# Two-layer trunk on one core: which splits stand behind tile 3's rows, and when the adaLN sums are split and multiplied

## The chip, the cores and the metric

One Trainium2 chip, one core. The metric is the device time of one execution in microseconds; before the change it is 1136.38 us (median of 3 runs, 1134.65 to 1137.98).

## What is computed

512 tokens of width 1024 pass through two layers, each a token mixer and then a SwiGLU feed-forward block (FFN):

```python
for i in range(2):
    shift, scale, gate = split(silu(c) @ mix_ada_w[i] + mix_ada_b[i], 3)
    h = rms_norm(x, mix_pre_g[i]) * (1 + scale) + shift
    y = stick_breaking_mixer(h) if i == 0 else token_mixing_mixer(h)   # attention / gMLP
    x = x + gate * rms_norm(y, mix_post_g[i])
    shift, scale, gate = split(silu(c) @ ffn_ada_w[i] + ffn_ada_b[i], 3)
    h = rms_norm(x, ffn_pre_g[i]) * (1 + scale) + shift
    y = (silu(h @ w_gate[i]) * (h @ w_up[i])) @ w_down[i]              # 1024 -> 2816 -> 1024
    x = x + gate * rms_norm(y, ffn_post_g[i])
```

Attention is stage 0, the first FFN stage 1 (FFN0 below), the gMLP stage 2, the second FFN stage 3 (FFN1). `shift`, `scale` and `gate` of a stage (the adaLN sums) are called `B`, `A` and `G` in the kernel. They hang on `c` alone and can be made at any time before the stage that uses them.

## The kernel before

**Arithmetic.** Every product runs in a rounded fp32 format. Each operand is split into a high and a low part: ACT writes the high part (`wh`, `as`, `hTh`, `acch`, with a copy), DVE writes the low part (`wl`, `hTl`, `accl`, with a subtraction of the two). `mm3` issues three matmuls, high x high, high x low, low x high. All matmuls are on line 88, transposes on 96, DVE and ACT instructions on 64, loads on 105, so groups are told apart by the names of their tiles.

**Tiling.** Tokens go in four tiles of 128 (0 to 3). In FFN0 and FFN1 the gate and up products run first, one unit of 128 hidden columns after another (`unit`, line 1022, for the first three units; `seven`, line 1040, for the other 19, a block scheme with 7 products whose weights are 2x2 block sums made in `blocks`, line 164). Then comes the down product, `out_proj` (line 468): k runs over 22 chunks of 128 hidden columns. Steps k = 0 to 17 do all four tiles, each step 24 matmuls of 128x512; the last four chunks (the tail) are done tile by tile, so that each tile's boundary can begin.

**Boundary.** `boundary` (line 395) turns one tile of `y` into the next stage's input: square sums on ACT, `t = y*G` and `x = t*r + x` on DVE, the new x out to DRAM, a square sum of x on ACT (`junk`), `t = x*A`, `t = t*r + B` on DVE, then eight transposes on TensorE (`tp<-pack,t`) and the splits of the transposed tile (`hTh`, `hTl`). Beside tiles 2 and 3 the first three units of the next stage (`nxt`, of two token tiles) are issued, so that TensorE has products while the boundary runs; the third (`nxt[2]`) is written after tile 3's boundary.

**adaLN sums.** `Bg` (line 295) is a generator. For each part (`A1`, `B1`, `G2`, ...) it loads eight 512 KB chunks of the adaLN weights (`rawada`) through a pool of two buffers on the SP queue and adds each to an accumulator 128x1024 on DVE (`A<-rawada,sc,A` and so on). Then, part by part and half by half (128x512), the accumulator is split (`acch`, `accl`), multiplied with a matrix of ones on TensorE into a PSUM bank (`adaps`), and evacuated back into the accumulator, with a gain vector `g` for A and G. A load is issued on SP only after the DVE instruction that frees its buffer, so it holds up the loads queued behind it. In FFN0's down product `bg` does two additions a step and the whole second half (`bg.step(99)`) at k = 12, for `A1`, `B1`, `G2`. At that point tile 0's running sum is put away in `yp`, and tile 0's two PSUM banks are given to `adaps`: from k = 13 tile 0 begins again (`y_` names with a new number), to be added to `yp` later. `bg2` makes `A2` and `B2`: their sums begin at k = 13 and are finished in the gMLP.

**What sets the order.** Behind the attention stage the instructions of each engine are ordered by the tile framework's scheduler: roughly in the order in which the program writes them, moved up where buffers are free. Buffers of the pool `s4` (28 slots of 4 KB a partition: x, sums, activations, `act`, and the split activations `as` of the down product) are handed out in the order in which the program asks. The weights of the down product go through six pairs `wh`, `wl` (pools of 5 and 1) and two raw buffers; a pair is written for step k + 6 when the last matmul of step k has read it.

Names and lines that the change touches: `Written` (55), `blocks` (164), `Bg` (295 to 363), `boundary` (395), `sums`, `out_proj` (468), `Ffn.first` (1022), and the place where `bg2` and `f0.run` are called.

Of the kernel before, what the change touches and what calls it, by code (L numbers as in the profile page):

```python
# [11 lines left out]
ALU = mybir.AluOpType  # L12
# [13 lines left out]
def trunk(ctx: ExitStack, tc: tile.TileContext, A: dict, out: bass.AP):  # L26
# [16 lines left out]
    def nm(s):  # L43
        uid[0] += 1
        return f"{s}_{uid[0]}"
# [9 lines left out]
    class Written:  # L55

        def __init__(self, engine):
            self.engine, self.prev, self.chain = engine, None, False

        def __getattr__(self, name):  # L60
            f = getattr(self.engine, name)

            def call(*a, **k):
                b = f(*a, **k)  # L64
                if self.chain and self.prev is not None:
                    order(b, self.prev)
                self.prev = b
                return b

            return call  # L70
# [97 lines left out]
    def blocks(xr, yr):  # L168

        fp = fwork["pool"]  # L170
        x = wtile(KD, P)
        split(x[0][:], x[1][:], xr[:])
        b21 = [fp.tile([P, 4, P], F32R, tag=f"b21{i}", name=nm("b21")) for i in range(2)]
        split(b21[0][:], b21[1][:], yr[:, 0:4, :])
        f13 = fp.tile([P, KD, P], F32, tag="f13", name=nm("f13"))
        dve.tensor_tensor(
            f13[:].rearrange("p (a k) f -> p a (k f)", a=2),
            xr[:].rearrange("p (a k) f -> p a (k f)", a=2),
            yr[:, 4:8, :].rearrange("p (a k) f -> p a (k f)", a=1).to_broadcast([P, 2, 512]),
            ALU.add,  # L180
        )
        t13 = wtile(KD, P)
        split(t13[0][:], t13[1][:], f13[:])
        f24 = fp.tile([P, KD, P], F32, tag="f24", bufs=1, name=nm("f24"))
        dve.tensor_tensor(f24[:, 0:4, :], f13[:, 0:4, :], xr[:, 4:8, :], ALU.add)
        dve.tensor_tensor(f24[:, 4:8, :], f24[:, 0:4, :], yr[:, 0:4, :], ALU.add)
        t24 = wtile(KD, P)
        split(t24[0][:], t24[1][:], f24[:])

        def half(t, i):  # L190
            return lambda k: (t[0][:, 4 * i + k, :], t[1][:, 4 * i + k, :])

        return {
            "B11": half(x, 0), "B22": half(x, 1), "B21": half(b21, 0),
            "T1": half(t13, 0), "T3": half(t13, 1), "T2": half(t24, 0), "T4": half(t24, 1),
        }
# [92 lines left out]
            acc, w, sc[:, kk : kk + 1], acc, ALU.mult, ALU.add  # L289
        )  # L290

    ada = {}

    class Bg:

# [1 line left out]

        def __init__(self, *parts, slots=False, queue=nc.sync):  # L300
            self.slots = slots
# [17 lines left out]
        def run(self):  # L319
            for name, at, s, part in self.parts:  # L320
                acc = slot(F32, name, 1, D)[:, 0, :]
                ada[name, at] = acc
                nc.gpsimd.memset(acc, 0.0)
                load(acc[0:1, :], A["adab"][s, part], self.queue)
                for k in range(KD):
                    if self.slots:
                        raw = slot(F32, "rawada", 1, D)[:, 0, :]
                        load(raw, A["ada"][s, part, k])
                        yield
                    else:  # L330
                        self.ahead(1 + (k + 1 < KD or name != self.parts[-1][0]))
                        raw = self.raws.pop(0)
                    ada_stt(acc, raw, k)
                    if not self.slots:
                        yield
            for name, at, s, part in self.parts:
                acc = ada[name, at]
                if part:
                    row = A["pre_g"] if part == 1 else A["post_g"]
                    g = slot(F32, "g", 1, D)[:, 0, :]  # L340
                    load(g, row[s : s + 1, :].to_broadcast([P, D]))
                for b in range(2):
                    c = slice(b * 512, (b + 1) * 512)
                    h = adas.tile([P, 512], F32R, tag="acch", name=nm("acch"))
                    l = adas.tile([P, 512], F32R, tag="accl", name=nm("accl"))
                    split(h[:], l[:], acc[:, c])
                    yield
                    yield
                    ps = self.bank()
                    mm(ps[:], ones_r, h[:], True, False, last_tp[0])  # L350
                    mm(ps[:], ones_r, l[:], False, True)
                    if part == 0:
                        act.activation(acc[:, c], ps[:], AF.Copy)
                    elif part == 1:
                        dve.scalar_tensor_tensor(acc[:, c], ps[:], 1.0, g[:, c], ALU.add, ALU.mult)
                    else:
                        dve.tensor_tensor(acc[:, c], ps[:], g[:, c], ALU.mult)

        def step(self, n=1):

# [30 lines left out]
    def boundary(s, tt, y, xin, hT, S, tag):  # L391
# [21 lines left out]
        sd, r1 = rms(sx[:])  # L413
        dve.tensor_tensor(t[:], x[:], ada["A", s], ALU.mult)
        dve.reciprocal(r1[:], sd[:])
        dve.scalar_tensor_tensor(t[:], t[:], r1[:, 0:1], ada["B", s], ALU.mult, ALU.add)
        late = []
        for q in range(2):
            ps = bank("tp", tag)
            for k in range(4):  # L420
                kk = q * 4 + k
                transpose(ps[:, k * P : (k + 1) * P], t[:, kk * P : (kk + 1) * P])
            a = ps[:].rearrange("p (a b) -> p a b", a=4)
            if tt % 2 == 0:
# [8 lines left out]
            late.append(a)  # L433
        return lambda: sums(S, tt, late)

    def sums(S, tt, a):

# [19 lines left out]
        part("3", f[:, 0])  # L457

    xd = {}

    def x_load(tt):

# [5 lines left out]
    def out_proj(s, nk, get_act, wkey, J, bg, hT, nxt=(), pre=None, S=None, steps=0, bg2=None):  # L468
# [23 lines left out]
        if pre is not None:  # L492
            npre = len(pre["w"])
            for tt in pre["y"]:
                y[tt] = pre["y"][tt]
        for k in range(nk - J):
            a = get_act(k)
            w = pre["w"][k] if k < npre else wget(wkey(k))
            for tt in range(NT):
                if k >= npre or tt not in pre["y"]:  # L500
                    step(k, tt, a, w)
            bg.step(steps)
            if bg2 is not None and mid is not None and k >= mid:
                bg2.step(1)
            if k + 1 == mid:
                yp = slot(F32, "yp")
                for hf in range(2):
                    act.activation(yp[:, hf, :], y[last][hf][:], AF.Copy)
                bg.step(99)
        bg.step(99)  # L510
        tail = [
            (k, get_act(k), wget(wkey(k), J + 1 if k == nk - J else 0))
# [17 lines left out]
        for n, tt in enumerate((2, 3)):  # L530
            if nxt:
                evacs.append(nxt[n]())
            late.append(boundary(s, tt, y[tt], xin, hT, S, "p" if tt == 3 else "b"))
        if nxt:
            evacs.append(nxt[2]())
            with tc.issue_after(last_sqrt[0].ins):
                for f in evacs:
                    f()
        if hT is not None:
            for f in late:  # L540
                f()

    def sqrt_table():
        with tc.issue_after(last_act[0].ins):
# [445 lines left out]
    class Ffn:  # L990
# [29 lines left out]
            return evac  # L1020

        def first(self):
            return [lambda f=f: self.unit(f, 0, 256, 2) for f in range(NH)]

        def seven(self, f):

# [90 lines left out]
    def gmlp(bg, hT, nhT, nS, nxt):  # L1117
# [112 lines left out]
        0, KD, lambda k: (o8[k][:, 0, :], o8[k][:, 1, :]), lambda k: ("wo", k),  # L1230
        4, bg, hT1, f0.first(), early, S1,
    )
    bg2 = Bg("A2", "B2")
    f0.run(
        Bg("G1", slots=True), Bg("A1", "B1", "G2"), bg2, 2, hT2,
        [lambda a=a: u_first(hT2, range(a, min(a + 2, NU))) for a in range(0, NU, 2)],
    )
    gmlp(bg2, hT2, hT3, S3, f1.first())
# [86 lines left out]
```

## Time and profile before

| what | value |
|---|---|
| median of 3 runs | 1136.38 us (1134.65 to 1137.98) |
| the profiled execution, its own time | 1136.57 us |
| its span in the profile | 1134.7 us |
| PE busy | 98% of the span |
| DVE, ACT, POOL busy | 74%, 51%, 4% |
| mean granted TensorE clock | 0.999 |

The profile is of one execution. Times in it are microseconds from the span's start; the execution's own time is 1.9 us longer than the span. A row of the timeline gives start, length, engine, line, instruction and tiles, how many such followed each other, and in brackets the idle time of the engine before it with what ended it.

### The profile page before, as it was taken

What the parts mean: (1) busy time and instruction counts of PE and PEld (TensorE: products, weight loads), DVE (VectorE), ACT (ScalarE), POOL (GpSimd) and SP (SyncE); (2) the same over time, 40 slices, a digit from 0 to 9 for tenths busy, and PEclk for the clock granted to TensorE, in tenths of its full rate; (3) what the DMA queues carried; (4) which work ended last, traced back from release to release, by engine and by line L of the source; (5) the groups of instructions that cost most, each with busy time, mean ns of one, the idle gap of its engine ahead of it and who ended that gap; (6) DMA issues with size and microseconds to landing.
All of it is one profiled execution on the core that took longest, in us unless ns stands there. A gap on an engine that the chain in (4) does not pass through costs nothing.

```text
span 1134.7 us, 17753 instructions
## 1 busy us (share of the span) xinstructions
PE 1114.4 (98%) x7120; PEld 989.6 (87%) x7120; DVE 842.1 (74%) x1077; ACT 573.7 (51%) x955; POOL 39.8 (4%) x71
## 2 busy tenths in 40 slices
PE   7999999999999999999999999999999999999997
PEld 5787878778999999988778978988999999988886
DVE  7777988769898988786687665669988888692214
ACT  7745767655555555561335534436555555571112
POOL 0211010000000000010000000000000000000000
PEclk9999999999999999999999999999999999999999
DMA  9676554354234444277873673333244444154312
GB/s 364 229 227 178 163 148 135 112 194 136 93 119 144 148 149 129 78 248 264 283 265 146 207 238 94 93 130 131 93 131 148 141 134 133 60 179 131 97 39 75
DMA packets 48481, 176.08 MB, mean 155 GB/s; under 512 B 5643, under 2 KB 6155, under 8 KB 47502
## 3 DMA queue, kind: packets, MB, share of 16 engines
q1 hardware_dynamic: 42350, 153.95, 41.9%
q0 software_dynamic: 6048, 20.98, 5.9%
q8 instruction: 56, 0.92, 0.3%
q14 instruction: 27, 0.22, 0.1%
HBM read 164.43 MB, written 8.39 MB: 152 GB/s over the span
## 4 chain that ended last, share of the span: by engine, by line
PE 78%; DMA 9%; DVE 9%; ACT 2%; issue 2%; SPq 0%; DVEq 0%; ACTq 0%
PE r L88 32%; PE y L88 21%; PE pqk L88 7%; DMA rawada<-in_ada 5%; PE v L88 5%; PE gu L88 4%; PE z L88 2%; PE u L88 2%; DVE wl L64 2%; PE tw L96 1%; PE av L88 1%; DMA ada<-in_ada0w 1%; DMA raw<-in_win_v 1%; DVE t L64 1%; PE sv L88 1%
## 5 line engine op out<-in xcount | busy, mean ns | idle before, releaser
L88 PE MATMUL y<-wh,as 128*128 128x512 f32 x832 | 264.4, 396 | 0.6 <-DVE G L64 0.6
L64 DVE TENSOR_TENSOR wl<-raw,wh 128x1024 fp32r<-128x1024 f32 (+1 forms) x112 | 135.2, 1212 | 112.7 <-ACT wh L64 112.3
L64 ACT ACTIVATE wh<-raw 128x1024 fp32r<-128x1024 f32 (+1 forms) x112 | 117.2, 1052 | 187.7 <-PE y L88 99.8
L88 PEld LDWEIGHTS y<-wh,as 128*128 128x128 f32 x832 | 156.2, 188 | 37.2 <-DVE G L64 1.0
L88 PE MATMUL r<-Sl,wh 128*128 128x256 f32 x608 | 170.5, 280 | 0.0
L88 PE MATMUL r<-Sh,wh 128*128 128x256 f32 x608 | 170.5, 280 | 0.0
L88 PE MATMUL r<-Sh,wl 128*128 128x256 f32 x608 | 170.3, 280 | 0.0
L88 PE MATMUL y<-wl,as 128*128 128x512 f32 x416 | 164.2, 395 | 0.0
L64 DVE TENSOR_TENSOR wl<-f,wh 128x1024 fp32r<-128x1024 f32 x76 | 92.9, 1222 | 37.2 <-ACT wh L64 37.1
L64 ACT ACTIVATE wh<-f 128x1024 fp32r<-128x1024 f32 x76 | 80.6, 1061 | 75.2 <-PE r L88 65.2
L88 PEld LDWEIGHTS r<-Sh,wh 128*128 128x128 f32 x608 | 114.8, 189 | 0.0
L88 PEld LDWEIGHTS r<-Sh,wl 128*128 128x128 f32 x608 | 114.8, 189 | 0.0
L88 PEld LDWEIGHTS r<-Sl,wh 128*128 128x128 f32 x608 | 114.7, 189 | 0.0
L88 PEld LDWEIGHTS y<-wl,as 128*128 128x128 f32 x416 | 78.1, 188 | 19.0
L88 PE MATMUL r<-hTh,wh 128*128 128x256 f32 x304 | 88.9, 293 | 0.1
L88 PE MATMUL r<-hTl,wh 128*128 128x256 f32 x304 | 85.1, 280 | 0.0
L88 PE MATMUL r<-hTh,wl 128*128 128x256 f32 x304 | 80.3, 280 | 0.0
L64 ACT ACTIVATE e<-r 128x256 f32<-128x256 f32 x114 | 43.5, 381 | 53.5 <-PE r L88 53.3
L88 PEld LDWEIGHTS r<-hTh,wh 128*128 128x128 f32 x304 | 57.2, 188 | 4.7 <-DVE gu L64 1.1
L88 PE MATMUL r<-hTh,b 128*128 128x256 f32 x304 | 60.7, 282 | 0.0
L64 ACT ACTIVATE wh<-rawx 128x1024 fp32r<-128x1024 f32 x38 | 40.3, 1062 | 34.0 <-PE r L88 31.0
L88 PEld LDWEIGHTS r<-hTl,wh 128*128 128x128 f32 x304 | 57.3, 188 | 0.1
(197 smaller groups left out, 2452.8 us busy)
## 6 DMA issues: line engine op xcount, KB each, us to landing
rawada<-in_ada SPq DMA_DIRECT2D x56, 512.0 KB, 4.9
raw<-in_wdown SPq DMA_DIRECT2D x44, 512.0 KB, 4.3
rawy<-in_wy SPq DMA_DIRECT2D x38, 512.0 KB, 3.6
rawx<-in_wx SPq DMA_DIRECT2D x38, 512.0 KB, 4.2
rawada<-in_ada POOLq DMA_DIRECT2D x24, 512.0 KB, 4.4
raw<-in_wqk SPq DMA_DIRECT2D x16, 512.0 KB, 4.0
ada<-in_ada0w SPq DMA_DIRECT2D x7, 1026.0 KB, 10.7
raw<-in_wgu SPq DMA_DIRECT2D x12, 512.0 KB, 3.6
```

The source lines that it names most:

```text
L64: b = f(*a, **k)
L88: b = nc.tensor.matmul(o, l, r, start=start, stop=stop, skip_group_check=True)
L96: last_tp[0] = nc.tensor.transpose(o, i, ident)
```

## The change

Three edits.

1. **A gate at the boundaries.** After both boundaries of tiles 2 and 3 are written, DVE and ACT instructions that follow (`dve.gate`, `act.gate`) are ordered behind tile 3's last `t` (DVE) and behind the last square root (ACT). Under this gate come tile 2's hT splits, now a function of their own (`turned`), and the whole of `nxt[2]` with the weight splits that it asks for. The sum `f13` of `blocks` is ordered behind the same `t`. `first` no longer asks for weights ahead at its second unit (`2 if f != 1 else 0`). These are orders within an engine; the same work is done.
2. **Sums split when complete (`hold=True`).** For `A1`, `B1`, `G2` and for `A2`, `B2` the split of an accumulator follows its eighth addition, once, 128x1024, into two slots of `s4` in place of the two small buffers of the pool `adas`. The slots are held until the part's products are done.
3. **Products one a step.** The burst after k = 12 becomes one product (two matmuls and the evacuation) per `bg` step, two a step of k. As `adaps` holds tile 0's banks for longer, tile 0's share of steps 13 and 14 is put off and done at k = 15. In the gMLP, where `bg2` is finished, the second half goes with the steps there.

The core of the diff:

```diff
@@ Bg.run
                     ada_stt(acc, raw, k)
+                    if k == KD - 1 and self.hold:
+                        held[name, at] = slot(F32R, "acch"), slot(F32R, "accl")
+                        split(*[t[:].rearrange("p a b -> p (a b)") for t in held[name, at]], acc)
                     if not self.slots:
                         yield
...
+            def finish():
+                s, part, acc, g, c, h, l = pending.pop(0)
+                ps = self.bank()
+                mm(ps[:], ones_r, h, True, False, last_tp[0])
+                mm(ps[:], ones_r, l, False, True)
...
                 for b in range(2):
                     c = slice(b * 512, (b + 1) * 512)
+                    if self.hold:
+                        pending.append((s, part, acc, g, c, *[t[:, b, :] for t in held[name, at]]))
+                        finish()
+                        yield
+                        continue
@@ boundary
-        dve.scalar_tensor_tensor(t[:], t[:], r1[:, 0:1], ada["B", s], ALU.mult, ALU.add)
+        ready[0] = dve.scalar_tensor_tensor(t[:], t[:], r1[:, 0:1], ada["B", s], ALU.mult, ALU.add)
...
+        if tt != 2:
+            turned(tt, hT, S, late)
+        return lambda: sums(S, tt, late), lambda: turned(tt, hT, S, late)
@@ out_proj
+                if mid is not None and tt == last and k >= mid:
+                    if k >= mid + 2:
+                        for j in put:
+                            step(j[0], tt, *j[1:])
+                elif k >= npre or tt not in pre["y"]:
                     step(k, tt, a, w)
-            bg.step(steps)
...
                     act.activation(yp[:, hf, :], y[last][hf][:], AF.Copy)
-                bg.step(99)
+            bg.step(steps)
...
         if nxt:
+            dve.gate, act.gate = ready[0], last_sqrt[0]
+            late[0][1]()
             evacs.append(nxt[2]())
+            dve.gate = act.gate = None
@@ Ffn.first, call
-            return [lambda f=f: self.unit(f, 0, 256, 2) for f in range(NH)]
+            return [lambda f=f: self.unit(f, 0, 256, 2 if f != 1 else 0) for f in range(NH)]
-    bg2 = Bg("A2", "B2")
+    bg2 = Bg("A2", "B2", hold=True)
-        Bg("G1", slots=True), Bg("A1", "B1", "G2"), bg2, 2, hT2,
+        Bg("G1", slots=True), Bg("A1", "B1", "G2", hold=True), bg2, 2, hT2,
```

How the rows stand on the engines at three places:

DVE at the end of the attention stage, before; `x_2258` is tile 3's new x, `t_2474` its normalised row, `wl` are weight splits of the third unit, `hTl_2399` and `hTl_2408` tile 2's low parts, `f` block sums:

```order
L64 SCALAR_TENSOR_TENSOR x_2258<-t_2474,r_2482,x_2258 128x1024
L64 TENSOR_TENSOR wl_2414<-raw_2411,wh_2413 128x1024
L64 TENSOR_TENSOR wl_2420<-raw_2417,wh_2419 128x1024
L64 TENSOR_TENSOR hTl_2399<-tp_2393,hTh_2398 128x4x128
L64 TENSOR_TENSOR hTl_2408<-tp_2402,hTh_2407 128x4x128
L64 TENSOR_TENSOR t_2474<-x_2258,A_944 128x1024
L64 RECIPROCAL r_2492<-sd_2490 128x1
L64 TENSOR_TENSOR f_427_2526<-rawx_2510,rawy_2511 128x1024
L64 SCALAR_TENSOR_TENSOR t_2474<-t_2474,r_2492,B_1396 128x1024
```

The same place after, where `t_2454` is tile 3's row and `b` are splits of the first block's weights:

```order
L64 SCALAR_TENSOR_TENSOR x_2258<-t_2454,r_2462,x_2258 128x1024
L64 TENSOR_TENSOR t_2454<-x_2258,A_944 128x1024
L64 RECIPROCAL r_2472<-sd_2470 128x1
L64 SCALAR_TENSOR_TENSOR t_2454<-t_2454,r_2472,B_1396 128x1024
L64 TENSOR_TENSOR wl_2501<-raw_2498,wh_2500 128x1024
L64 TENSOR_TENSOR wl_2507<-raw_2504,wh_2506 128x1024
L64 TENSOR_TENSOR b_426_2523<-rawy_2511,b_425_2522 128x512
L64 TENSOR_TENSOR b_438_2548<-rawy_2515,b_437_2547 128x512
L64 TENSOR_TENSOR hTl_2487<-tp_2393,hTh_2486 128x4x128
```

The five instructions between x and the last t are behind it now, and two block splits have joined them.

ACT in FFN0's down product, before, at the end of the gate and up products; `as_5499` is the split activation of step k = 8, `as_5656` that of k = 12:

```order
L64 ACTIVATE as_5499<-act_3541 128x512
L64 ACTIVATE as_5541<-act_3541 128x512
L64 ACTIVATE as_5580<-act_3791 128x512
L64 ACTIVATE as_5619<-act_3791 128x512
L64 ACTIVATE gu_5061<-r_788_5057 128x256
L64 ACTIVATE as_5656<-act_4044 128x512
L545 ACT_TABLE_LOAD
```

After, the same splits are `as_5507` (k = 8) to `as_5627` (k = 11) and `as_5668` (k = 12). They stand behind this table load, eight instructions and more into the down product; `acch_5503` and `acch_5664` are the new splits of the sums `B1` and `G2`, `wh_5593` and `wh_5762` weights of steps 13 and 17, whose buffers the last matmuls of steps 7 and 11 set free:

```order
L64 ACTIVATE acch_5503<-B_5377 128x1024
L64 ACTIVATE wh_5593<-raw_5591 128x1024
L64 ACTIVATE as_5507<-act_3541 128x512
L64 ACTIVATE as_5549<-act_3541 128x512
L64 ACTIVATE as_5588<-act_3791 128x512
L64 ACTIVATE as_5627<-act_3791 128x512
L64 ACTIVATE wh_5632<-raw_5630 128x1024
L64 ACTIVATE wh_5673<-raw_5671 128x1024
L64 ACTIVATE wh_5719<-raw_5717 128x1024
L64 ACTIVATE acch_5664<-G_5540 128x1024
L64 ACTIVATE wh_5762<-raw_5760 128x1024
L64 ACTIVATE as_5668<-act_4044 128x512
```

The splits of steps 4 to 7, 8 to 11 and from 12 on now stand behind the splits of `A1`, `B1` and `G2` in turn (on DVE alike), where before the ones up to step 12 were done ahead of the down product's bulk.

SP in the gMLP, before; `g_6668` is the gain vector for `A2`, `rawada` are chunks of `B2`:

```order
L105 DMA B_6583<-in_adab 1x1024
L105 DMA raw_6544<-in_win_v 128x1024
L105 DMA g_6668<-in_pre_g 128x1024
L105 DMA raw_6589<-in_win_v 128x1024
L105 DMA rawada_6607<-in_ada 128x1024
L105 DMA rawada_6610<-in_ada 128x1024
```

After, `g_6664` is the same vector, `rawada_6644` the last chunk of `B2`, `rawy` raw weights of FFN1's first blocks, loaded into the buffers of the last two chunks:

```order
L107 DMA rawada_6644<-in_ada 128x1024
L107 DMA rawy_7743<-in_wy 128x1024
L107 DMA raw_6780<-in_win_u 128x1024
L107 DMA rawy_7747<-in_wy 128x1024
L107 DMA g_6664<-in_pre_g 128x1024
L107 DMA raw_6786<-in_win_u 128x1024
```

The load of g is issued behind the second `rawy` now, which waits for the last addition into `B2`.

More of the change, by code (lines that the diff above doesn't have):

```diff
@@ L57, in __init__ @@
         def __init__(self, engine):
-            self.engine, self.prev, self.chain = engine, None, False
+            self.engine, self.prev, self.chain, self.gate = engine, None, False, None
         def __getattr__(self, name):
@@ L66, in call @@
                     order(b, self.prev)
+                if self.gate is not None:
+                    order(b, self.gate)
                 self.prev = b
@@ L175, in blocks @@
         f13 = fp.tile([P, KD, P], F32, tag="f13", name=nm("f13"))
-        dve.tensor_tensor(
+        add = dve.tensor_tensor(
             f13[:].rearrange("p (a k) f -> p a (k f)", a=2),
@@ L181, in blocks @@
         )
+        order(add, ready[0])
         t13 = wtile(KD, P)
@@ L290, in ada_stt, with __init__ @@
         )
-    ada = {}
+    ada, held = {}, {}
     class Bg:
-        def __init__(self, *parts, slots=False, queue=nc.sync):
-            self.slots = slots
+        def __init__(self, *parts, slots=False, hold=False, queue=nc.sync):
+            self.slots, self.hold = slots, hold
             self.queue = queue
@@ L333, in run @@
                     ada_stt(acc, raw, k)
+                    if k == KD - 1 and self.hold:
+                        held[name, at] = slot(F32R, "acch"), slot(F32R, "accl")
+                        split(*[t[:].rearrange("p a b -> p (a b)") for t in held[name, at]], acc)
                     if not self.slots:
                         yield
+            pending = []
+            def finish():
[3 more added lines that the diff above has]
+                mm(ps[:], ones_r, l, False, True)
+                if part == 0:
+                    act.activation(acc[:, c], ps[:], AF.Copy)
+                elif part == 1:
+                    dve.scalar_tensor_tensor(acc[:, c], ps[:], 1.0, g[:, c], ALU.add, ALU.mult)
+                else:
+                    dve.tensor_tensor(acc[:, c], ps[:], g[:, c], ALU.mult)
             for name, at, s, part in self.parts:
-                acc = ada[name, at]
+                acc, g = ada[name, at], None
                 if part:
@@ L346, in run @@
                     split(h[:], l[:], acc[:, c])
+                    pending.append((s, part, acc, g, c, h[:], l[:]))
                     yield
                     yield
[L349 to L357, printed above, removed]
+                    finish()
         def step(self, n=1):
@@ L422, in boundary, with turned @@
                 transpose(ps[:, k * P : (k + 1) * P], t[:, kk * P : (kk + 1) * P])
-            a = ps[:].rearrange("p (a b) -> p a b", a=4)
-            if tt % 2 == 0:
+            late.append(ps[:].rearrange("p (a b) -> p a b", a=4))
+        if tt != 2:
+            turned(tt, hT, S, late)
+        return lambda: sums(S, tt, late), lambda: turned(tt, hT, S, late)
+    def turned(tt, hT, S, late):
+        for q, a in enumerate(late):
+            if (tt // 2, q) not in hT:
                 hT[tt // 2, q] = (slot(F32R, "hTh", 4, 256), slot(F32R, "hTl", 4, 256))
@@ L432, in boundary @@
                 act.activation(S["c", q][:, :, tt * P : (tt + 1) * P], a, AF.Copy)
-            late.append(a)
-        return lambda: sums(S, tt, late)
     def sums(S, tt, a):
@@ L459, in trunk @@
     xd = {}
+    ready = [None]
     def x_load(tt):
@@ L495, in out_proj @@
                 y[tt] = pre["y"][tt]
+        put = []
         for k in range(nk - J):
@@ L498, in out_proj @@
             w = pre["w"][k] if k < npre else wget(wkey(k))
+            put.append((k, a, w))
             for tt in range(NT):
-                if k >= npre or tt not in pre["y"]:
+                if mid is not None and tt == last and k >= mid:
[3 more added lines that the diff above has]
+                elif k >= npre or tt not in pre["y"]:
                     step(k, tt, a, w)
-            bg.step(steps)
+            if mid is None or k + 1 < mid or k >= mid + 2:
+                put = []
             if bg2 is not None and mid is not None and k >= mid:
@@ L505, in out_proj @@
             if k + 1 == mid:
+                put = []
                 yp = slot(F32, "yp")
@@ L540, in out_proj @@
             for f in late:
-                f()
+                f[0]()
     def sqrt_table():
```

## The prediction

> **What bounds the kernel now.** I read the page's busy times first, then the waits of PE, then the timelines of DVE, ACT and SP at the places that the change touches.
>
> ```profile
> span 1134.7 us, 17753 instructions
> PE 1114.4 (98%) x7120; PEld 989.6 (87%) x7120; DVE 842.1 (74%) x1077; ACT 573.7 (51%) x955; POOL 39.8 (4%) x71
> PE tp L96 <- DVE t L64: 2.5, 3, 1.5
> PE adaps L88 <- ACT acch L64: 1.9, 2, 1.4
> PE y L88 <- DVE G L64: 0.6, 1, 0.6
> PE adaps L88 <- DVE accl L64: 0.2, 1, 0.2
> ```
>
> TensorE is the bound: 1134.7 less 1114.4 leaves 20.3 us in which it doesn't multiply. The four rows of its waits (us in total, times, longest) are those that the change can end: the transposes of tile 3 waiting for `t` at three boundaries, and the adaLN products waiting for splits and banks; together 5.2 us. Each wait costs a little more than its idle time:
>
> ```profile
> 566.39 0.62 PE L88 MATMUL y<-wh,as 128*128 128x512 f32 x2
> 568.46 0.50 PE L88 MATMUL adaps<-acch,ones 128*128 128x512 f32 x1 [1.45 <-ACT acch L64]
> 568.80 0.40 PE L88 MATMUL y<-wl,as 128*128 128x512 f32 x1
> ```
>
> 568.46 less 566.39 is 2.07 us for two matmuls. Two take 0.47 where nothing waits (24 take 5.60, below), so 1.60 is lost against 1.45 of idle: 0.15 for the restart. Seven waits make 1.1 us, so **at most 5.2 + 1.1 = 6.3 us can be gained**, 0.55% of the run. 0.3% of the time, 3.4 us, is about what a measurement of this kernel can tell from no change.
>
> **Part 1, the gate (3.0 of the 6.3 us).** The longest of the three waits for `t`, at the end of attention:
>
> ```profile
> 266.67 1.28 DVE L64 SCALAR_TENSOR_TENSOR x<-t,r,x 128x1024 f32<-128x1024 f32 x1
> 268.16 1.06 ACT L64 ACTIVATE wh<-raw 128x1024 fp32r<-128x1024 f32 x1 [1.80 <-DMA raw<-in_wgu]
> 269.25 2.49 DVE L64 TENSOR_TENSOR wl<-raw,wh 128x1024 fp32r<-128x1024 f32 x2 [1.30 <-ACT wh L64]
> 273.13 1.22 DVE L64 TENSOR_TENSOR t<-x,A 128x1024 f32<-128x1024 f32 x1
> 275.46 1.28 DVE L64 SCALAR_TENSOR_TENSOR t<-t,r,B 128x1024 f32<-128x1024 f32 x1
> 275.00 0.28 PE L88 MATMUL gu<-hTh,wl 128*128 128x256 f32 x1
> 276.79 0.66 PE L96 MATMUL tp<-pack,t 128*128 128x128 f32 x4 [1.51 <-DVE t L64]
> ```
>
> Tile 3's x is there at 267.95, yet its `t` starts only at 273.13: in between DVE waits for a weight load through ACT and does two `wl` and two `hTl`. In the new order `t` is next behind x: 1.22 and 1.28 for the two, some 0.5 between them for ACT's square sum and root, so they end near 271, where they ended at 276.74. The transposes stand behind the second unit on PE, whose last matmul started at 275.00; nothing is waited for. The same holds at the two later boundaries, so the 2.5 us and three restarts go. What comes behind t pays: two `wl`, four `hTl` and two block splits move into a stretch where DVE is already full, 19.70 of 20 us:
>
> ```profile
> 280.00:300.00 20.00, 20.00 (x172) 20.00 (x171) 19.70 (x30) 10.66 (x17) 0.00 (x0) 1.00 0.30 89
> ```
>
> PE never waits there now, and what is added is 1.25 us of DVE work, done up to then in idle time. Were all of it uncovered it would cost 1.3 us at each of the two SwiGLU boundaries; the block's products do not need the two splits first, so I take 0.1 each, 0.2 us in all, bounds 0 and 0.6 in the range.
>
> **Part 2, sums split when complete.** This is where I expect the loss. Rows of before, in the down product of FFN0:
>
> ```profile
> 494.41 0.62 ACT L64 ACTIVATE as<-act 128x512 fp32r<-128x512 f32 x1
> 495.05 1.28 ACT L545 ACT_TABLE_LOAD   x1
> 510.89 1.28 DVE L64 SCALAR_TENSOR_TENSOR A<-rawada,sc,A 128x1024 f32<-128x1024 f32 x1
> 514.25 0.63 PE L88 MATMUL y<-wh,as 128*128 128x512 f32 x2
> 514.74 1.06 ACT L64 ACTIVATE wh<-raw 128x1024 fp32r<-128x1024 f32 x1 [1.90 <-PE y L88]
> 515.03 1.28 DVE L64 SCALAR_TENSOR_TENSOR B<-rawada,sc,B 128x1024 f32<-128x1024 f32 x1
> 521.16 1.28 DVE L64 SCALAR_TENSOR_TENSOR B<-rawada,sc,B 128x1024 f32<-128x1024 f32 x1 [2.11 <-DMA rawada<-in_ada]
> 526.66 1.28 DVE L64 SCALAR_TENSOR_TENSOR B<-rawada,sc,B 128x1024 f32<-128x1024 f32 x1 [1.19 <-DMA rawada<-in_ada]
> 531.54 1.06 ACT L64 ACTIVATE wh<-raw 128x1024 fp32r<-128x1024 f32 x1 [4.54 <-PE y L88]
> 532.56 1.29 DVE L64 SCALAR_TENSOR_TENSOR B<-rawada,sc,B 128x1024 f32<-128x1024 f32 x1 [1.52 <-DMA rawada<-in_ada]
> 534.10 1.28 DVE L64 SCALAR_TENSOR_TENSOR B<-rawada,sc,B 128x1024 f32<-128x1024 f32 x1 [0.26 <-DMA rawada<-in_ada]
> 538.34 1.28 DVE L64 SCALAR_TENSOR_TENSOR G<-rawada,sc,G 128x1024 f32<-128x1024 f32 x1 [1.82 <-DMA rawada<-in_ada]
> 559.52 1.28 DVE L64 SCALAR_TENSOR_TENSOR G<-rawada,sc,G 128x1024 f32<-128x1024 f32 x1 [1.63 <-DMA rawada<-in_ada]
> 562.82 3.75 ACT L64 ACTIVATE as<-act 128x512 fp32r<-128x512 f32 x7
> 563.48 3.70 DVE L64 TENSOR_TENSOR as<-act,as 128x512 fp32r<-128x512 f32 x6 [0.26 <-ACT as L64]
> ```
>
> By 495 ACT has split the activations up to step 12; from then on it only follows PE: (531.54 - 514.74) / 3 = 5.60 us, one step of k (24 matmuls). These `wh` wait for the last matmul of steps 3 and 6. The PE row holds step 3's last matmul and step 4's first: the one starts at 514.25 and lets `wh` go at 514.74, the other starts 0.23 behind it, 514.5. So k = 4 is due at 514.5, k = 8 at 514.5 + 4 x 5.60 = 536.9, k = 12 at 559.3, and a `wh` that waits for the end of a step starts 0.25 after the next step is due.
>
> In the new order each group of four `as` stands behind the split of a sum, and for k = 8 and 12 behind a `wh` as well, which waits for the end of the step just before (the order of ACT in the section on the change). So k = 8 needs, one after another on ACT: the end of B1's eighth addition, `acch` (about 1.0), `wh` (0.95 apart), one `as` (3.75 / 7 = 0.53), 0.1 for the signal. The low parts, on DVE, are covered by the seven products with the high part that stand first in that step.
>
> - **k = 4.** A's last addition ends at 512.17, as before; + 1.0 + 0.5 + 0.1 = 513.8, due 514.5. Cost 0, upper bound 0.5.
> - **k = 8.** B's first addition comes later: behind 512.17 stand a `wl` (1.2), `accl` 128x1024 (1.2), four `as` (3.70 / 6 = 0.61 each), another `wl` (1.2), so 518.2 in place of 515.03. From there the chain of two buffers sets the pace: an addition frees a buffer, the load is issued, lands, is added. Before it took 532.56 - 515.03 = 17.5 us for three rounds, one round 5.5 at the fastest (521.16 to 526.66). B's eighth addition then ends at 518.2 + 17.5 + 1.5 + 1.3 = 538.5, at the fastest pace 537.2. Plus 2.6: 541.1 or 539.8, due 536.9. **Wait 2.9 to 4.2; I take 3.8**, as only one round was at the fastest pace. Even with the sum in time, `wh` behind the step's end makes 0.25 + 0.95 + 0.53 + 0.1 = 1.85.
> - **k = 12.** G starts behind `accl`, `wl` and four `as` (1.2 + 1.2 + 2.4 behind 539.5): 544.4, not 538.34. Its eight took 559.52 + 1.28 - 538.34 = 22.5 us before, 20.3 at B's pace (17.5 + 1.5 + 1.3). They end at 564.7 or 566.9; plus 2.6 is 567.3 or 569.5, due 559.3 + 3.8 = 563.1. With three rounds of 5.5 for B and G both, G starts at 543.1, takes 19.0 and the step is ready at 564.7, due 559.3 + 2.9. **Wait 2.5 to 6.0; I take 4.0, near B's pace**; the least is 1.85 again.
>
> **Part 3, products one a step.** The waits for `acch`, `accl` and `G` go (2.7 us and four restarts, the rest of the 6.3): the splits are long done, and a step lies between an evacuation and the next use of its bank. Tile 0's put-off steps only trade places. But in the gMLP the order of SP moves:
>
> ```profile
> 644.63 0.42 SPq L105 DMA_DIRECT2D g<-in_pre_g  x1
> 670.88 0.33 SPq L105 DMA_DIRECT2D rawy<-in_wy  x1
> 672.82 0.40 PE L88 MATMUL adaps<-acch,ones 128*128 128x512 f32 x1
> 674.20 0.68 DVE L64 SCALAR_TENSOR_TENSOR A<-adaps,g 128x512 f32<-128x512 f32 x1
> DMA to landing us min/median/max: 6.6/6.6/6.6
> DMA to landing us min/median/max: 3.5/4.6/9.9
> ```
>
> `g` was issued at 644.63, 28 us ahead of its use. Now it stands behind the second `rawy`, which waits for B2's last addition (670.88): issued at 671.3. The last two rows are for `g` (6.6, one sample) and `rawada` (4.6): it lands at 677.9 or 675.9, at 674.8 by the fastest. `A<-adaps,g` takes 0.68, then its bank is free for the third product, which stands nine matmuls (2.1 us) behind the place of the 672.82 row: due 674.9. **Wait 0.7 to 3.8; I take 2.3.** Two waits of 0.2 and 0.4 that stood nearby are among the gains.
>
> **The sum**, against the profiled execution's 1136.57: - 6.3 + 0.2 + 0 + 3.8 + 4.0 + 2.3 = + 4.0, so 1140.6; the median stands 0.2 lower, **1140.4**.
>
> **The rivals.**
>
> *Not slower: the row loads keep up.* The mechanism is the landing time of `rawada` in FFN0's down product. At the 3.5 us minimum of the row above a round is 1.3 + 0.3 + 3.5 = 5.1, three are 15.3, and B ends at 518.2 + 15.3 + 1.2 + 1.3 = 536.0: its split ends at 537.0, when `wh` is just released (531.54 + 5.60). G starts 2.4 + 1.2 + 1.2 behind that, 541.9, and ends 15.3 + 2.5 later, 559.7; k = 12 is due at 559.3 + 1.85 and its `wh` released at 561.4. So only 1.85 is left at each, and g costs 0.7: - 6.3 + 3.7 + 0.7 + 0.2 = - 1.7, 1134.7. It decides where the eighth additions end a microsecond ahead of the release of `wh`, 536.1 and 560.4. For it: loads that no longer wait for DVE find freer queues. Against: no round in the rows is under 5.5. Chance 0.28.
>
> *Slower still: PE comes back slow after the long wait.* If the array fell to half its pace in a wait of 4 us, and needed as long to come back, two such waits would cost 2.0 more each: + 4.0, 1144.4. The longest wait in the rows above is 1.5 us, with 0.15 lost at the restart and a granted clock of 1.00 in the window, so no row speaks for it, and none reaches as far. Chance 0.07. [...]
>
> *Slower still: tile 3's t is not freed* (ACT's square sum or a load is late all the same): the 2.5 us and three restarts stay, + 3.0, 1143.4. Against: x is on DVE at 267.95 and ACT is idle from 266.35 to 268.16. Chance 0.05.
>
> *Faster by over 0.3%:* it would need the waits at k = 8, k = 12 and g together under 2.9, less than two releases of `wh` (3.7). I see no mechanism; 0.05 for an error in reading the order.
>
> **Chances and range.** Forecast 0.55, the rivals 0.28, 0.07, 0.05 and 0.05. The forecast's own bounds go from - 6.3 + 2.9 + 2.5 + 0.7 = - 0.2 to - 6.3 + 0.6 + 0.5 + 4.2 + 6.0 + 3.8 = + 8.8, 1136.2 to 1145.2. With the first rival below and the slow ones above taken in by 0.7 to 0.8 us at either end, the range is 1134.0 to 1146.0. Slower by over 0.3% (above 1139.8): 0.42 of the forecast's 0.55 and both slow rivals, 0.54. Within: 0.13 of the forecast and 0.23 of the first rival, 0.36. Faster: the rest of that rival and the last one, 0.10.
>
> **What would show it.** Right: PE waits for ACT `as` twice in FFN0's down product, at k = 8 and at k = 12, 2.5 to 6 us each; `B` additions there begin about 3 us later relative to PE; one wait of `adaps` for DVE `A` in the gMLP, with `g` issued right behind `rawy`; the waits for `t`, `acch` and `G` gone. Wrong: no wait for `as`, or one of under 1.5 us; sums that end before the step is due; a wait left at `tp`.

## The result, and the profile after

| | before | after |
|---|---|---|
| median | 1136.88 us (4 runs) | 1146.85 us (1144.52 to 1148.76, 4 runs) |
| ratio, 95% interval | | 1.0089 (1.0072 to 1.0105) |
| profiled execution, its span | 1136.57, 1134.7 | 1147.02, 1145.3 |
| mean granted TensorE clock | 0.999 | 0.995 |

The changed kernel is slower, by 8 to 12 us: the sign that was forecast, 6.4 us above the number and 0.85 us above the range's upper end. The waits of PE in the profile after (us in total, times, longest), of which the first two are new:

```profile
PE y L90 <- ACT as L64: 7.2, 2, 3.9
PE adaps L90 <- DVE A L64: 3.1, 1, 3.1
PE v L90 <- ACT hTh L64: 2.6, 3, 1.5
```

The waits for `t`, `acch`, `accl` and `G` are gone. `as` is waited for at k = 8 and k = 12, the bank of A2 in the gMLP once (line 90 is line 88 of before). At k = 8 the rows of the two engines on which it hangs, DVE (B's first, third, fifth, seventh and eighth addition) and ACT:

```profile
518.79 2.60 DVE L64 SCALAR_TENSOR_TENSOR B<-rawada,sc,B 128x1024 f32<-128x1024 f32 x2
524.60 1.29 DVE L64 SCALAR_TENSOR_TENSOR B<-rawada,sc,B 128x1024 f32<-128x1024 f32 x1 [0.80 <-DMA rawada<-in_ada]
530.14 1.29 DVE L64 SCALAR_TENSOR_TENSOR B<-rawada,sc,B 128x1024 f32<-128x1024 f32 x1 [0.74 <-DMA rawada<-in_ada]
535.96 1.29 DVE L64 SCALAR_TENSOR_TENSOR B<-rawada,sc,B 128x1024 f32<-128x1024 f32 x1 [0.95 <-DMA rawada<-in_ada]
538.09 1.28 DVE L64 SCALAR_TENSOR_TENSOR B<-rawada,sc,B 128x1024 f32<-128x1024 f32 x1 [0.85 <-DMA rawada<-in_ada]
```

```profile
539.41 1.06 ACT L64 ACTIVATE acch<-B 128x1024 fp32r<-128x1024 f32 x1 [5.67 <-DVE B L64]
540.37 1.04 ACT L64 ACTIVATE wh<-raw 128x1024 fp32r<-128x1024 f32 x1
541.32 2.18 ACT L64 ACTIVATE as<-act 128x512 fp32r<-128x512 f32 x4
```

And PE, with what had not been forecast behind the wait:

```profile
537.69 0.39 PE L90 MATMUL y<-wh,as 128*128 128x512 f32 x1
541.99 0.51 PE L90 MATMUL y<-wh,as 128*128 128x512 f32 x1 [3.91 <-ACT as L64]
542.33 0.40 PE L90 MATMUL y<-wl,as 128*128 128x512 f32 x1
542.56 0.40 PE L90 MATMUL y<-wh,as 128*128 128x512 f32 x1
...
543.71 1.91 PE L90 MATMUL y<-wh,as 128*128 128x512 f32 x4
545.42 0.63 PE L90 MATMUL y<-wl,as 128*128 128x512 f32 x1
...
546.90 0.63 PE L90 MATMUL y<-wh,as 128*128 128x512 f32 x2
547.37 0.39 PE L90 MATMUL y<-wl,as 128*128 128x512 f32 x1
```

The chain is the one of the prediction: the sum is late, its split, one `wh` and `as` follow on ACT, and PE stands for 3.91 us. Then, from 1.3 us behind the restart on, matmuls are slow: the four from 543.71 take 545.42 - 543.71 = 1.71 us, 0.43 each where 0.23 is usual. By 546.9 the pace is back. The granted clock says the same (columns behind the stretch: its length, then PE, PEld, DVE, ACT, POOL busy, then PEclk, the granted clock; the last two are the DMA engines' share and GB/s):

```profile
530.00:537.00 7.00, 7.00 (x32) 5.69 (x31) 4.84 (x4) 1.06 (x1) 0.00 (x0) 1.00 0.79 269
542.00:547.00 5.00, 5.00 (x15) 3.96 (x16) 4.96 (x7) 1.50 (x3) 0.00 (x0) 0.66 0.47 145
569.00:574.00 5.00, 4.56 (x13) 3.61 (x14) 1.91 (x3) 2.01 (x5) 0.00 (x0) 0.66 0.74 242
687.00:691.00 4.00, 4.00 (x12) 3.17 (x13) 2.18 (x4) 2.08 (x4) 0.00 (x0) 0.63 0.02 7
```

All three long waits (3.91, 3.24 and 3.08 us) are followed by such a stretch. Restart included, the matmuls behind them take 1.65, 1.65 and 1.54 us more than at 0.233 us each: 4.84 us that no wait shows.

Where the time lies: every trace has 7120 matmuls, so the n-th of one can be set beside the n-th of before. What each stretch took more than in the profile of before (us; `k = 8` is from k = 4 to 10, `k = 12` from there to 15, `tile 0` the steps behind, where its banks are taken back):

| profile | start to 271 us | end of attention | k = 8 | k = 12 | tile 0 | to gMLP | gMLP | to FFN1 | whole |
|---|---|---|---|---|---|---|---|---|---|
| after | 2.7 | -1.7 | 5.8 | 3.3 | -0.8 | -0.7 | 3.2 | -1.0 | 10.5 |
| after, second profile | 1.8 | -1.7 | 5.4 | 4.8 | -0.8 | -0.7 | 5.7 | -1.0 | 13.2 |
| gate alone | 3.2 | -1.7 | 0.0 | -1.4 | 0.1 | -0.7 | -1.6 | -1.0 | -3.4 |
| gate alone, second | 0.6 | -1.7 | 0.0 | -0.7 | -0.6 | -0.7 | -1.6 | -1.0 | -6.0 |
| held sums alone | 3.1 | 0.2 | 7.1 | 3.4 | -0.7 | 0.2 | 1.6 | -0.2 | 14.2 |
| as ahead | -0.1 | -1.7 | 0.0 | 5.5 | -0.9 | -0.7 | 0.6 | -1.0 | 1.5 |
| as ahead, g early | 0.7 | -1.7 | 0.0 | 5.6 | -0.7 | -0.7 | 0.6 | -1.0 | 2.7 |
| A1 late | 0.4 | -1.7 | 2.1 | 3.1 | -0.8 | -0.7 | 4.1 | -1.0 | 5.2 |
| three buffers | 0.0 | -1.7 | 0.0 | -0.2 | 3.8 | -0.7 | -1.6 | -1.0 | -1.4 |
| late split | 2.8 | -1.7 | 0.0 | -1.8 | 3.9 | -0.7 | -1.6 | -1.0 | 0.3 |

(Stretches of under 0.7 us are left out, so rows do not add up to the last column exactly.) In the first column TensorE does the same work in the same order in every kernel, and the column moves from -0.1 to 3.2; so the 2.7 us at the start of the profile after are not shown to be part of the change. Of the 3.2 and 3.1 of the gate alone and the held sums alone, some 1.4 us each are slow matmuls behind a wait for `qlow` at 90 us (2.13 and 1.84 us). Each row is one execution. The one of `as ahead` is the fastest of eight, 4.7 us under their median, so it shows less than that kernel's usual loss.

### The profile page after: what moved, and what is told of

It is laid out like the page before. It is cut to its first block, busy times and chain, and to the rows that moved or that the text cites. A ratio compares the mean times of both kernels' runs of the same rounds, so it can differ in the third digit from the quotient of the medians.

```text
span 1145.3 us, 17741 instructions
## 1 busy us (share of the span) xinstructions
PE 1116.1 (97%) x7120; PEld 990.9 (87%) x7120; DVE 842.2 (74%) x1072; ACT 573.8 (50%) x950; POOL 39.8 (3%) x71
## 4 chain that ended last, share of the span: by engine, by line
PE 46%; DMA 3%; DVE 1%; issue 1%; ACT 1%; DVEq 0%; SPq 0%; ACTq 0%
PE y L90 20%; PE r L90 17%; PE gu L90 3%; PE u L90 2%; DMA rawada<-in_ada 2%; PE v L90 2%; PE sv L90 1%; PE tp L98 1%; PE adaps L90 0%; DVE B L64 0%; DVE G L64 0%; DMA g<-in_pre_g 0%; DMA raw<-in_win_v 0%; ACT wh L64 0%; ACT as L64 0%
```

## The experiments

**Gate alone** (two times) and **held sums alone**. The diff cut in two: the first has `Written.gate`, `turned`, the orders behind `ready[0]` and the look-ahead, the second `hold=True`, the products one a step and tile 0's put-off steps.

> The gate alone (hT splits of tile 2 and the third unit behind tile 3's t, f13 behind t, the look-ahead of the second unit), sums and products as before. Theory A (three waits of PE made by the held sums, each followed by a stretch at half pace): no wait for as, no stretch of 0.43 us matmuls, the three waits for t gone; 3.3 us less at the boundaries, 0.3 more at one unit: about 1133.9 against 1136.9. Theory B (part of the loss belongs to the gate or to the start of the kernel, where PE was 2.8 us later in the profile after): 1136 or more, and the start late again.

> Sums split when complete and products one a step, without the gate. Theory A: the three waits (4.1, 3.4 and 3.4 us) and the stretches at half pace (1.3 to 1.5 us each) as in the profile after, the boundaries as before: 3 us more than the whole change, about 1147 to 1150. Theory B: under 1145.

> The gate alone, again, on the same chip as e9. Both theories: 3 to 4 us under the kernel before. If e9 repairs all of it, e9 is at most 1 us away from this; if products one a step cost of their own, e9 is 2 us or more above it.

Measured: gate alone 1133.21 us, ratio 0.9973 (0.9957 to 0.9989), and on another chip 1132.03, ratio 0.9953 (0.9935 to 0.9971): faster than both kernels. Held sums alone 1147.73, ratio 1.0100 (1.0081 to 1.0119). Both are as theory A has it. The halves hardly touch each other: the boundary columns belong to the first, k = 8 and 12 to the second. The three waits for `t` stay in the second:

```profile
PE y L88 <- ACT as L64: 8.2, 2, 4.9
PE adaps L88 <- DVE A L64: 2.9, 1, 2.9
PE tp L96 <- DVE t L64: 2.6, 3, 1.7
```

That the start is late in the first profile of the gate alone too (3.2) and not in the second (0.6) goes against theory B.

**The whole change again**, unchanged.

> The whole change once more, for a second profile. Theory A: three waits of 3 to 4 us with seven or eight matmuls of 0.43 us behind each; the first 100 us, which the change does not touch, late against before by something between 0 and 3 us as loads land (so not the change's); 1145 to 1148. Theory B (the start is late because of the change): again 2.8 us late at the same places.

1146.76 us, ratio 1.0081 (1.0059 to 1.0103). The same three waits, 3.83, 3.53 and 4.51 us, each with its slow stretch (1.46, 2.90 and 2.63 us with the restart). The start was 1.8 us late here, so it varies.

**Activations asked for ahead**, and the same with **g early**:

```diff
-            a = get_act(k)
+            while len(acts) < min(k + (6 if steps else 1), nk - J):
+                acts.append(get_act(len(acts)))
+            a = acts[k]
```
```diff
+                        if part:
+                            gs[name, at] = slot(F32, "g", 1, D)[:, 0, :]
+                            row = A["pre_g"] if part == 1 else A["post_g"]
+                            load(gs[name, at], row[s : s + 1, :].to_broadcast([P, D]))
```

> The whole change, but in the down product of FFN0 the activations are asked for (and so split) up to six steps ahead, so that those of k = 8 to 12 stand ahead of the splits of B1 and G2. Theory A: the waits at k = 8 and k = 12 and the half pace behind them go, 10.4 us; the wait for g in the gMLP stays, with its stretch: about 1134 to 1136. Theory B1 (the matmuls of 0.43 us are slow for another reason, such as the loads beside them): the waits go, the slow matmuls near k = 8 and 12 stay: 3 us more, 1137 to 1139. Theory B2 (the splits are not what PE waits for): no gain, 1145 or more.

> As e3, and g loaded when its sum is complete, ahead of the next sum's chunks. Theory A: all three waits and all half pace gone, the gains of the change left: 7 us less than before, 1129 to 1131, and no stretch of 0.43 us matmuls. Theory B1: 1133 to 1135 with such stretches left. Theory B2: 1140 or more.

1142.67 us, ratio 1.0047 (1.0033 to 1.0061), and 1138.67, ratio 1.0016 (1.0007 to 1.0026): less loss than the whole change, but no gain over before. Both waits for `as` are gone, with their slow matmuls, so the splits were what PE waited for. But a new one stood behind them, at the end of k = 12; ACT and PE of the kernel with activations ahead:

```profile
567.66 1.06 ACT L64 ACTIVATE acch<-G 128x1024 fp32r<-128x1024 f32 x1 [8.95 <-DVE G L64]
...
569.57 0.61 ACT L64 ACTIVATE as<-act 128x512 fp32r<-128x512 f32 x1
570.09 1.06 ACT L64 ACTIVATE yp<-y 128x512 f32<-128x512 f32 x2
```

```profile
565.54 0.39 PE L90 MATMUL y<-wh,as 128*128 128x512 f32 x1
570.72 0.79 PE L90 MATMUL adaps<-acch,ones 128*128 128x512 f32 x1 [4.79 <-ACT yp L64]
571.31 0.63 PE L90 MATMUL adaps<-accl,ones 128*128 128x512 f32 x1
571.74 0.63 PE L90 MATMUL adaps<-acch,ones 128*128 128x512 f32 x1
```

ACT stands 8.95 us before the split of G2, and the copies that free tile 0's banks queue behind it. In the change this was hidden: `as` of k = 12 waited in the same place. Neither theory had named it, and the times expected were missed by it (4.79 us and a stretch at 0.43 us a matmul). The profiled execution with activations ahead took 1137.98 us at a clock of 0.997; the other seven took 1141.27 to 1144.30 at 0.992 to 0.996. What they lost besides, no trace shows. Theory B1 falls: where no wait is, at k = 8, no matmul is slow. In the gMLP g early ended the wait for g (1.98 us without, none with it); 1.27 us for `accl` of B2 took its place.

**G2's split behind the copies** (put off to where the products reach B1), with both edits above for FFN0 and the sums of the gMLP as before:

```diff
-                    if k == KD - 1 and self.hold:
+                    if k == KD - 1 and self.hold and name == self.parts[-1][0]:
+                        last.append((name, at, acc))
+                    elif k == KD - 1 and self.hold:
...
-    bg2 = Bg("A2", "B2", hold=True)
+    bg2 = Bg("A2", "B2")
```

> The whole change with three repairs in FFN0's down product: activations asked for up to six steps ahead (as in e3), A's g loaded when its sum is complete, and G2's split moved behind the copies into yp at k = 12; A2 and B2 in the gMLP are split as before the change. Theory (what costs is that splits which wait for a late sum stand on ACT ahead of copies that PE needs: as in the change, yp in e3 and e5): no wait of PE over 1 us from k = 0 to 17 and no stretch at half pace; about the gate alone, 1132 to 1134. Rival (the one-a-step products or tile 0's put-off steps cost something of their own): a wait left near k = 13 to 15, 1136 or more.

1138.13 us, ratio 1.0003 (0.9987 to 1.0018), where the gate alone on the same chip made 1132.03. The wait for `yp` is gone; one of 2.95 us is left, for `G` (tile 0's banks), again with slow matmuls behind it. So the rival is right in that a wait of its own is left, worth 4 us in the column of tile 0. The lateness of the sums is not its reason: the kernel with three buffers below has the same wait with earlier sums. Which part of the change makes it isn't settled by a run; in both traces G's evacuation on DVE stands behind additions of A2, and in the one with three buffers DVE waited 1.05 us for the chunk of one.

**A1 split and multiplied as before** (`if k == KD - 1 and self.hold and name + str(at) != "A1"`), the rest of the change as it is.

> The whole change, but A1's sum is split and multiplied as before (two halves, through the small buffers, behind k = 12), so B's additions start 3 us earlier and the chains are shorter. Theory A, by its durations: at k = 8 a wait of about 1.1 us (B's eighth addition ends at 535.4, split 1.0, one wh 0.95, as 0.5), at k = 12 one of about 2.8; half pace behind neither, if it needs a wait of more than about 3.4 us. Rival (half pace follows every wait): slow matmuls behind both.

1141.71 us, one execution. At k = 8 0.77 us for `as` and 0.80 for its low part (1.1 expected), without slow matmuls; at k = 12 3.06 (2.8 expected), with seven of them. So slow matmuls follow neither every wait nor only those over 3.4 us, and both guesses miss. B's later start did come from the rows that A's held split put ahead of it.

**Three buffers for the chunks** (a third `raw2`, up to three loads ahead, 27 slots in place of 28: with 28 the third buffer does not fit, 24.5 of the 26 KB a partition that a later pool needs are left).

> The whole change with three buffers in place of two for the adaLN chunks, and 27 slots in place of 28 to make room. If the landing time of the chunks (the two-buffer chain) sets when the sums are complete, B's eighth addition ends 1 to 3 us earlier against PE and the waits at k = 8 and k = 12 fall to between 0 and 2 us, with no half pace behind them; if something else does (loads sharing the queue), the waits stay at 3 to 4.

1135.11 us, one execution: 11.7 us less than the change. B's eighth addition begins 7 us earlier against PE, where 1 to 3 were expected (538.09 in the change, with PE 2.6 us later there), and PE waits 0.26 us for ACT and 0.80 for DVE at k = 12, not at all at k = 8:

```profile
528.30 1.29 DVE L64 SCALAR_TENSOR_TENSOR B<-rawada,sc,B 128x1024 f32<-128x1024 f32 x1 [2.16 <-DMA rawada<-in_ada]
554.25 1.28 DVE L64 SCALAR_TENSOR_TENSOR G<-rawada,sc,G 128x1024 f32<-128x1024 f32 x1 [2.03 <-DMA rawada<-in_ada]
```

So the chain of two buffers set when the sums were complete. (With 27 slots the order moved a little too: the `wh` between split and `as` went, 1 us of the 3.9; 27 slots alone were not run.) What is left is a wait of 3.07 us for `G`, as in the kernel with G2's split behind the copies.

**Waits put in by hand**, into the kernel before, in the down product of FFN1, where no sums run:

```diff
+            if s == 3 and k in DOSE:
+                dve.tensor_scalar(d[:], y[3][1][:, 0:1], 0.0, None, ALU.mult)
+                for _ in range(DOSE[k]):
+                    nc.gpsimd.tensor_scalar(a[0], a[0].bitcast(F32), d[:, 0:1], None, ALU.add)
```

> The kernel before with six waits of PE put into the down product of the last FFN, at k = 2, 5, 8, 11, 14, 17: a column of y read when the step before is done, then 1, 2, 3, 4, 5, 7 passes of GpSimd over that step's high parts, adding zero. Nothing else changes there. Theory A with a clock gate: waits of under about 3 us cost only themselves and 0.15 us, longer ones are followed by a stretch of 3 to 4 us at 0.43 us a matmul, 1.3 to 1.6 us more each. Rival (the slow stretches come from the loads of the adaLN sums): no slow matmuls, since no sums run there.

> As e8, with waits near the point in question: one pass over 64 columns (a warm-up), then 512, 512 + 192, 512 + 256, 512 + 320, 512 + 448 columns. By e8 a pass of 512 takes 1.65 us and the wait is 0.4 more, so about 2.1, 2.7, 2.9, 3.2 and 3.6 us. Theory A (gate with a threshold): no slow matmuls behind 2.1 and 2.7, 8 to 12 of them behind 3.2 and 3.6. Rival (the loss grows in proportion to the wait): some slow ones behind each.

The passes took about 1.65 us, so the six waits of the first were 3.83 to 11.98 us (the one of a single pass was 5.26, as that pass, GpSimd's first for over 200 us, took 4.20). Behind the shortest:

```profile
1041.27 0.79 PE L89 MATMUL y<-wh,as 128*128 128x512 f32 x1 [3.83 <-POOL as L504]
1041.86 0.63 PE L89 MATMUL y<-wl,as 128*128 128x512 f32 x1
1042.29 1.05 PE L89 MATMUL y<-wh,as 128*128 128x512 f32 x2
```
```profile
1026.00:1032.00 6.00, 6.00 (x28) 4.82 (x27) 1.23 (x1) 1.19 (x2) 0.00 (x0) 1.00 0.28 87
1042.00:1045.00 3.00, 3.00 (x9) 2.32 (x8) 0.00 (x0) 0.00 (x0) 0.00 (x0) 0.50 0.25 96
```

Clock 0.50, with the loads at 96 GB/s against 87 in the stretch at full clock: the slow stretch follows the wait, not the sums. Restart included it took 2.03, 2.52, 2.10, 2.60, 2.19 and 2.02 us more than the usual pace, whether the wait was 4 or 12 us.

In the second kernel three of the longer passes came as two waits, one of about 2.0 us and a shorter one 1 us behind. Its single wait of 1.98 us was followed by slow matmuls, which theory A had not expected there, and the loss did not grow with the wait, as the rival would have it.

Over all traces, single waits of 3.04 us or more (21 of them, the first wait of each kernel left out) all had a slow stretch, those of up to 1.71 none. Between, 1.84, 1.98, 2.13 and 2.95 had one, 1.98 and 2.91 had none, so the length alone does not decide.

The granted clock shows more. In the profile after it has three stretches at 0.50 before the last 1.3 us, each 3.41 us long, one behind each long wait. Each pair of rows below is the 3.41 us ahead of a stretch and the stretch itself; the first row is the 3.41 us in which the wait of 3.91 us begins:

```profile
536.38:539.79 3.41, 1.69 (x8) 1.08 (x6) 2.15 (x2) 0.38 (x1) 0.00 (x0) 1.00 0.81 268
539.80:543.21 3.41, 1.23 (x5) 1.04 (x6) 2.71 (x3) 3.41 (x6) 0.00 (x0) 1.00 0.71 228
543.21:546.62 3.41, 3.41 (x9) 2.66 (x9) 3.37 (x6) 0.29 (x1) 0.00 (x0) 0.50 0.54 156
...
567.10:570.51 3.41, 1.07 (x5) 0.89 (x6) 2.56 (x3) 2.29 (x3) 0.00 (x0) 1.00 0.82 285
570.52:573.93 3.41, 3.41 (x10) 2.64 (x9) 0.39 (x1) 1.55 (x4) 0.00 (x0) 0.50 0.73 211
...
683.16:686.57 3.41, 0.54 (x3) 0.10 (x1) 1.25 (x3) 0.60 (x1) 0.00 (x0) 1.00 0.94 316
686.57:689.98 3.41, 3.21 (x8) 2.59 (x9) 1.95 (x4) 1.35 (x3) 0.00 (x0) 0.50 0.08 32
```

In the 3.41 us ahead of the stretches TensorE stood idle for 3.41 - 1.23 = 2.18, 2.34 and 2.87 us; the 3.41 - 1.69 = 1.72 us of the first row were followed by 1.00. With held sums alone, the wait of 2.91 us lies in two such rows, 3.41 - 1.83 = 1.58 us in the one and 3.41 - 2.08 = 1.33 in the next, and the clock stays at 1.00:

```profile
685.78:689.19 3.41, 1.83 (x8) 1.13 (x6) 1.67 (x3) 0.99 (x3) 0.00 (x0) 1.00 0.89 310
689.20:692.61 3.41, 2.08 (x9) 1.74 (x10) 2.38 (x5) 1.46 (x3) 0.00 (x0) 1.00 0.26 102
692.61:696.02 3.41, 3.41 (x17) 2.75 (x16) 2.66 (x4) 2.63 (x4) 0.00 (x0) 1.00 0.02 5
```

The wait of 1.98 us in the second kernel lies within one row, and the next is at 0.50:

```profile
1034.64:1038.05 3.41, 1.43 (x7) 0.99 (x6) 1.38 (x2) 1.06 (x1) 1.56 (x1) 1.00 0.02 10
1038.06:1041.47 3.41, 3.41 (x10) 2.62 (x9) 0.00 (x0) 0.00 (x0) 0.00 (x0) 0.50 0.54 159
```

So in these rows half clock went with the idle time of the 3.41 us ahead of it, 1.98 us or more (1.72 and less were followed by 1.00), and not with the whole length of the wait. No row here lies between 1.72 and 1.98 us, and what places the stretches in time is not shown.

## Why the prediction was wrong

- **The gains.** Gate: 3.0 us forecast with 0.2 against it; - 1.7, - 0.7 and - 1.0 measured, 3.4. Right. The waits for `acch`, `accl` and `G` went as well. But the gate alone lost most of those too (- 1.4 or - 0.7 at k = 12, - 1.6 in the gMLP), and where the kernel before ran unchanged, in the two kernels with waits put in, k = 12 took 0.7 and 0.9 us less and the gMLP 0.4 and 0.6: part of these waits was that one profile's.
- **k = 4: nothing.** Right.
- **k = 8.** 2.9 to 4.2 forecast, 3.8 taken; 3.91. B began at 518.79 (518.2), its eighth addition ended at 539.4 (538.5), rounds of 5.5 to 5.8 us. Right, and three buffers show that the chain is the reason.
- **k = 12.** 2.5 to 6.0, 4.0 taken; 3.24. Right, though the slow matmuls behind k = 8 had made this step due 1.65 us later: without them the same sum would have been waited for about 4.9 us, an estimate from these two figures.
- **g in the gMLP.** 0.7 to 3.8, 2.3 taken; 3.08, and 4.51 in the second profile. `g` was issued at 680.69 behind the second `rawy`, as forecast. DVE, which waits for it, went on at 685.94, so it took at most 5.3 us to land; the trace has no landing of its own for this load (the 6.6 us that the prediction used are of another `g`, that of G2). Right, a little low.
- **The clock: the step that failed.** The three waits come to 10.2 us, where 10.1 were forecast; with the gains that makes the forecast's + 4. What the sum lacks is the 4.84 us of restarts and slow matmuls behind them: + 8.8, inside the measured 8.2 to 11.9. The sum put this at nothing. It stood among the rivals as "PE comes back slow after the long wait", priced at 2.0 us for each of two waits and 1144.4, with a chance of 0.07 because no row of before showed a wait as long. The price was near (1.5 to 1.7 for each of three) and the chance wrong: a trace whose waits behind the start end at 1.5 us can say nothing against it, while the forecast itself made three long ones.
- **The range.** It took that rival in only as far as 1146.0, as the upper end of two separate cases. The forecast's own upper waits and the clock belong together: behind all 21 waits of 3.04 us or more there was a slow stretch, behind none of up to 1.71.
- **"The row loads keep up"**, the rival on the other side (0.28): no, with two buffers no round fell under 5.5 us. The run with three buffers shows that sums which come sooner do end the waits for `as`, but that its 1135.1 us lie so near the rival's 1134.7 is luck: the rival had 1.85 us left at k = 8 and at k = 12 and 0.7 for `g`, the run has none, 1.06 and none, and 3.8 us more in the column of tile 0, which the rival did not have.

What stays open is G's late evacuation in the two repaired kernels, what the slower executions with activations ahead lose, and a microsecond or two of the difference of the medians.

## What to carry to other kernels

A split that follows a slow sum looks free because its engine is idle, but on an engine that works in order it holds up every copy queued behind it (with activations ahead ACT stood 8.95 us before the split of G2, and PE 4.79 us for the `yp` behind it): read in the order of the program built what stands behind an instruction that will wait. Price a wait of PE at its length and, where it is long, some 1.4 to 2.9 us more: here that came behind all 21 waits of 3.04 us or more and four of six between 1.84 and 2.95 us. And take a change with several parts apart: here one half was worth 3 to 5 us and the other cost 11.

## What the runs showed of the hardware

- In the profile after, TensorE's granted clock was 1.00 from 7.32 us on, but for three stretches at 0.50, each 3.41 us long, behind its three long waits, and the last 1.3 us. In the 3.41 us ahead of the three, TensorE stood idle for 2.18, 2.34 and 2.87 us. In the second kernel with waits put in, 1.98 us within 3.41 us were followed by 0.50; in the profile after, 1.72 us were followed by 1.00.
- A wait followed by a clock of 0.50 cost 1.4 to 2.9 us beyond its length, restart included; for the six waits of 3.83 to 11.98 us put in by hand it was 2.02 to 2.60 us, without growing with the length. In these stretches a matmul of 128x512 took 0.43 us in place of 0.23 (543.71 to 545.42 us of the profile after).
- A third buffer for 512 KB chunks (with one slot of 28 less) brought the eighth addition forward by 7 us, with the same queue and the same bytes; one execution.
- The first 271 us, the same work of TensorE in the same order, took between 0.1 us less and 3.2 us more than in the profile of before, over twelve profiles.
